# Gate and attention as one loop: a larger head start for the gate products, fewer of them per item, stored heads loaded three items ahead, and ScalarE's order written out

## The chip, the cores and the metric

The kernel runs on one core of one Trainium2 chip. The metric is the device time of one execution in microseconds (us). The core has TensorE (PE; its weight loads are shown as PEld), VectorE (DVE), ScalarE (ACT), GpSimd (POOL) and SyncE (SP), which here only issues DMAs. Each works through its own queue in order and waits on semaphores that the others set.

## The reference, cut to what matters

One step of a model with two layers, for 128 context tokens and 512 latent tokens of width 2048. The change lies in layer 0, the attention layer, and in the vectors for layer 1:

```
shift, scale, gate = split(silu(cond) @ w_mod[l] + b_mod[l])        # 2 condition rows
h = rms_norm(y, g_pre[l]) * (1 + scale) + shift
q, k, v, g = split(h @ w_in, [2048, 2560, 3072])                    # 16 heads of q, 4 of k and v
q, k = rope(rms_norm(q)), rope(rms_norm(k))                         # per head of 128
o = softmax(q @ [cache_k, k].T * HEAD_DIM ** -0.5) @ [cache_v, v]
out = (o * silu(g)) @ w_out                                         # g: one gate value per attention output
```

Latent tokens attend over 768 keys (256 cached and 512 of their own), context tokens over 128. Everything is float32.

## The kernel before

**Precision.** A float32 operand is split into two float32r parts. `split_w` casts a weight tile on ScalarE (L178, `wh`) and takes the difference on VectorE (L179, `wl`); both parts come out of a ring with a few slots. A product is then three float32r matmuls (`mm3`, L183 to L185). The activations lie in `hi` and `lo`, 128 x 16 x 642 each.

**Order.** Weights come through a ring of `raw` tiles of 1 MB, loaded by SyncE; a load waits until the last reader of its slot is done. TensorE follows the program's order inside the merged loop (`manual_schedule`). The other engines' queues are set by a scheduler that goes by priorities, and `split_w` asks for a high one.

**Ahead of the loop.** The gemms for k and q (`gemm_nat`) end with the last column blocks of q at 434 us. `gemv(0, ...)` runs in the background there. It accumulates the layer-1 shift on VectorE (L393, L395) in blocks of 1024 columns. At each of the two block ends, 16 float32 matmuls of 128x2 with `sel` (L402, 32 records in the trace) turn the sums over partitions into columns, and VectorE adds the bias (L409).

**The merged loop (L722 to L759).** `gate()` is a generator of 1536 products of 322 columns (L544): 16 heads, two halves of the tokens, two halves of the weights, 8 row blocks, three parts. It loads the gate weights of one head (L519) and calls `split_w` twice per head. `fill(n)` takes n products from it. The attention goes over 72 items: 16 heads by 4 blocks of 128 latent tokens, and after every odd head one item for the context tokens of two heads. Item n of the loop does the scores of item n and their softmax (`stage_s`: maximum L614, exponential L617, scaling L622 on ScalarE or L624 on VectorE), FILL[0] products, the weighted values of item n-2 (`stage_v`), FILL[1] products, the transposes of item n-1 (`stage_t`: L659, cast L662, difference L663), and FILL[2] products. Ahead of item 0, LEAD products are taken, all but 12 of them before the key and query transposes of head 0 (L576, L603). LEAD + 25 per item ends the gate with item 59.

**Where the results go.** `put_y` multiplies the attention output with the gate (L685). While the gate still runs, `hi` and `lo` hold its input, and a finished head is stored to DRAM (`a_s`, L699 on POOL's queue): heads 0 to 12. When it has ended (`over`), `put_y` writes `hi` on ScalarE (L687) and `lo` on POOL (L688) directly: heads 13 to 15. `load_a`, once per item from then on, brings one stored head back: load (L710), copy to `hi` on ScalarE (L711), difference to `lo` on POOL (L712). After the loop the output projection (`out_proj`) begins, a `gemm_nat` over `hi` and `lo` with `w_out_attn`, loaded by `load_w` (L169). Beside it, `gate_cols` sets its sums to zero on POOL (L773) and loads `w_mod`, `g_post` and `b_mod`.

## Time and profile before

| | us |
|---|---|
| three runs | 1981.70, 1983.51, 1984.18 |
| median | 1983.51 |
| the profiled execution | 1984.99 |
| its span in the trace | 1983.2 |
| TensorE busy in it | 1893.8 |

The profile is that of one execution. A line of order of time tells when an instruction started, how long it took and, in brackets, how long its engine had been idle before it and what ended that idle time. The table of windows cuts the span into stretches and tells for each how long every engine was busy and which TensorE clock was granted, as a share of full speed. Consecutive matmuls overlap in the records, so that the distance between starts, not the duration, tells what one costs. The loop starts after 434 us and the output projection starts at 910.92 us.

### The profile page before, as it was taken

The page shows a single profiled execution, that of the slowest core. Times are in us where ns is not written, and L with a number is a line of the kernel's source. Part 1 is how long each engine was busy: PE and PEld are TensorE (multiplying, and loading weights), DVE is VectorE, ACT ScalarE, POOL GpSimd, SP SyncE. Part 2 cuts the span into 40 slices and gives each one's busy share as a digit, 9 for nine tenths or more (in the row PEclk, how much of TensorE's full clock was granted, in tenths as well). Part 3 has the DMA queues.
Part 4 walks back from the last instruction along what each step waited for, and adds up shares of the span by engine and source line. Part 5 has one row for each costly group of instructions (what it writes and reads, how often), then busy time and mean ns, then how long its engine had stood idle before and what let it go on. Part 6 is the DMA issues. An engine that isn't in the chain of part 4 may idle for free.

```text
span 1983.2 us, 26998 instructions
## 1 busy us (share of the span) xinstructions
PE 1893.8 (95%) x10921; PEld 1693.3 (85%) x10921; DVE 1328.0 (67%) x1930; ACT 860.0 (43%) x1257; POOL 135.2 (7%) x215
## 2 busy tenths in 40 slices
PE   4999999998999999979999989999999999999997
PEld 1567888888999999977888889999999999987885
DVE  3237757848668685857867776775775674798645
ACT  4441222224444444463222555775365456642232
POOL 0000000000000000040000000100110010020000
PEclk9999999998999999999999989999999999999998
DMA  9995524624324252343555674322322322536445
GB/s 341 344 324 184 178 93 159 194 86 127 108 89 134 84 153 70 118 159 133 175 175 175 218 254 145 103 92 93 120 93 84 106 79 83 172 119 216 152 149 213
DMA packets 214701, 302.21 MB, mean 152 GB/s; under 512 B 7136, under 2 KB 140896, under 8 KB 211760
## 3 DMA queue, kind: packets, MB, share of 16 engines
q1 hardware_dynamic: 208848, 275.20, 42.8%
q0 software_dynamic: 5728, 25.28, 3.4%
q8 instruction: 86, 1.41, 0.3%
q14 instruction: 39, 0.32, 0.0%
HBM read 272.03 MB, written 28.42 MB: 151 GB/s over the span
## 4 chain that ended last, share of the span: by engine, by line
PE 75%; issue 11%; ACT 5%; DVE 5%; DMA 2%; SPq 1%; POOL 1%; DVEq 0%; ACTq 0%; POOLq 0%
PE pd L183 18%; PE pd L184 18%; PE pd L185 18%; PE pg L544 5%; PE pd L214 2%; PE pd L216 2%; PE pd L217 2%; PE pm L275 2%; PE pg L183 1%; ACT L976 1%; PE pg L185 1%; PE pg L184 1%; PE ph L659 1%; DVE wl L179 1%; PE ph L184 1%
## 5 line engine op out<-in xcount | busy, mean ns | idle before, releaser
L178 ACT CAST wh<-raw 128x1024 fp32r<-128x1024 f32 x248 | 258.7, 1048 | 527.8 <-PE pd L185 373.0
L179 DVE TENSOR_TENSOR wl<-raw,wh 128x1024 fp32r<-128x1024 f32 x248 | 301.9, 1221 | 218.4 <-ACT wh L178 217.2
L183 PE MATMUL pd<-wh,hi 128*128 128x512 f32 x1040 | 412.1, 396 | 8.0 <-ACT qf L485 3.8
L184 PE MATMUL pd<-wl,hi 128*128 128x512 f32 x1040 | 410.7, 395 | 0.0
L185 PE MATMUL pd<-wh,lo 128*128 128x512 f32 x1040 | 410.7, 395 | 0.0
L183 PEld LDWEIGHTS pd<-wh,hi 128*128 128x128 f32 x1040 | 196.1, 189 | 54.5 <-ACT qf L485 4.3
L183 PE MATMUL pd<-hi,wh 128*128 128x322 f32 x768 | 239.6, 312 | 0.0
L184 PE MATMUL pd<-lo,wh 128*128 128x322 f32 x768 | 238.4, 310 | 0.0
L185 PE MATMUL pd<-hi,wl 128*128 128x322 f32 x768 | 238.0, 310 | 0.0
L185 PEld LDWEIGHTS pd<-wh,lo 128*128 128x128 f32 x1040 | 196.1, 189 | 46.3
L184 PEld LDWEIGHTS pd<-wl,hi 128*128 128x128 f32 x1040 | 196.3, 189 | 45.4
L780 DVE SCALAR_TENSOR_TENSOR ga<-raw,cT,ga 128x512 f32<-128x512 f32 x256 | 175.5, 745 | 19.1 <-DMA ga<-b_mod 16.8
L395 DVE SCALAR_TENSOR_TENSOR ga<-raw,cT,ga 128x512 f32<-128x512 f32 (+1 forms) x180 | 162.5, 931 | 12.8 <-DMA raw<-w_mod 12.6
L544 PE MATMUL pg<-hi,wl 128*128 128x322 f32 x512 | 163.3, 319 | 0.0
L544 PE MATMUL pg<-lo,wh 128*128 128x322 f32 x512 | 162.9, 318 | 0.0
L544 PE MATMUL pg<-hi,wh 128*128 128x322 f32 x512 | 162.5, 317 | 0.0
L184 PEld LDWEIGHTS pd<-lo,wh 128*128 128x128 f32 x768 | 145.3, 189 | 0.0
L183 PEld LDWEIGHTS pd<-hi,wh 128*128 128x128 f32 x768 | 144.9, 189 | 0.1
L185 PEld LDWEIGHTS pd<-hi,wl 128*128 128x128 f32 x768 | 145.0, 189 | 0.0
L617 ACT ACTIVATE P<-sp,mx 128x768 f32<-128x768 f32 (+1 forms) x80 | 63.6, 797 | 98.3 <-DVE mx L614 98.3
L544 PEld LDWEIGHTS pg<-hi,wl 128*128 128x128 f32 x512 | 98.5, 192 | 0.0
L544 PEld LDWEIGHTS pg<-hi,wh 128*128 128x128 f32 x512 | 98.4, 192 | 0.0
(235 smaller groups left out, 3309.8 us busy)
## 6 DMA issues: line engine op xcount, KB each, us to landing
raw<-w_mod SPq DMA_DIRECT2D x64, 1024.0 KB, 5.2
raw<-w_in_lru SPq DMA_DIRECT2D x40, 1024.0 KB, 5.3
raw<-w_in_attn SPq DMA_DIRECT2D x36, 1024.0 KB, 5.8
raw<-w_mod SPq DMA_DIRECT2D x64, 512.0 KB, 8.1
raw<-w_out_attn SPq DMA_DIRECT2D x20, 1024.0 KB, 5.3
raw<-w_out_lru SPq DMA_DIRECT2D x20, 1024.0 KB, 6.1
y_s<-R POOLq DMA_DIRECT2D x16, 321.0 KB, 2.7
raw<-y_s SPq DMA_DIRECT2D x16, 321.0 KB, 4.2
```

The lines of the kernel that those rows point to most:

```text
L178: S.copy(wh, src)
L179: V.tensor_tensor(wl, src, wh.bitcast(F32), op=sub)
L183: PE.matmul(out, ah, bh, start=first, stop=False)
L184: PE.matmul(out, ah, bl, start=False, stop=False)
L185: PE.matmul(out, al, bh, start=False, stop=last)
L214: PE.matmul(outs[f], wh[:, c], hi[:, k, t], start=(k == 0 and first[f]), stop=False, skip_group_check=True)
L216: PE.matmul(outs[f], wh[:, c], lo[:, k, t], start=False, stop=False, skip_group_check=True)
L217: PE.matmul(outs[f], wl[:, c], hi[:, k, t], start=False, stop=(k == KT - 1), skip_group_check=True)
L395: V.scalar_tensor_tensor(acc[c], wk[:, k2], cT[:, k, c:c + 1], acc[c], op0=mult, op1=add)
L544: PE.matmul(acc[:, :TH], x[:, c], y[:, k, t], start=(q == 0 and k8 == 0 and n == 0), stop=(q == 1 and k8 == 7 and n == 2))
L617: S.activation(dst, src, AF.Exp, bias=mx[:, j:j + 1], accum_out=sm[:, j:j + 1])
L780: V.scalar_tensor_tensor(acc[:, c], raw[:, k4 * 512:k4 * 512 + 512], cT[:, kb * 4 + k4, c:c + 1], acc[:, c], op0=mult, op1=add)
```

## The change

Five edits:

- `LEAD` goes from 44 to 104 and `FILL` from (9, 8, 8) to (8, 8, 7). The gate then ends in the first fill of item 62 instead of with item 59, and one more head, 13, is stored and loaded back.
- `gemv(0, ...)` splits its two sums with `split_w` and takes 32 float32r matmuls (L405) in place of 16 float32 ones at each block end.
- `load_a` loads one stored head per item, up to three items ahead of the copy. It loads only heads that have been stored, and stops at the first head that went directly. With 14 stored heads, eight are copied in the rounds 65 to 72 of the loop over items, one in the last round, 73, and five in the loop behind it.
- ScalarE is added to `manual_schedule`: in the merged loop its queue is in the program's order too.
- The loop behind the items runs until nothing is left to load or copy.

```diff
--- before.py
+++ after.py
@@ -32,8 +32,8 @@
 QSCALE = HD ** -0.5
 NORM = "dadad"
 GGB = 5
-LEAD = 44
-FILL = (9, 8, 8)
+LEAD = 104
+FILL = (8, 8, 7)
 GATE2 = (1, 2, 5)
 GATE1 = (3, 4, 5, 6)
 NB1 = 2
@@ -397,10 +397,13 @@
                     if k2 % 2 or nk == 2:
                         yield
             pg = ps_()
+            parts = [split_w(a) for a in acc] if part == 0 else [(a,) for a in acc]
             for k in range(nf):
-                for c in range(2):
-                    PE.matmul(pg[:, 2 * k:2 * k + 2], acc[c][:, k * 128:k * 128 + 128],
-                              sel[:, c].bitcast(F32), start=(c == 0), stop=(c == 1))
+                ks = slice(k * 128, k * 128 + 128)
+                todo = [(a[:, ks], c) for c in range(2) for a in parts[c]]
+                for j, (a, c) in enumerate(todo):
+                    PE.matmul(pg[:, 2 * k:2 * k + 2], a, sel[:, c] if part == 0 else sel[:, c].bitcast(F32),
+                              start=(j == 0), stop=(j == len(todo) - 1))
             kt = col // 128
             src = pg[:, :2 * nf].rearrange("p (k c) -> p c k", c=2)
             b0 = 80 + part * 16 + kt
@@ -508,7 +511,7 @@
     def psh():
         return psH.tile([128, 512], F32, name="ph", tag="ph")
 
-    ggs, over, direct = {}, [], {}
+    ggs, over, direct, stored = {}, [], {}, set()
 
     def gate():
 
@@ -697,19 +700,25 @@
                 put_y(h - 1 + e, slice(PO, TE), po[:, e * 128:e * 128 + 128])
                 if not direct[h - 1 + e]:
                     G.dma_start(a_s[h - 1 + e][:, :TE], ggs[h - 1 + e][:, :TE])
-
-    back = iter(range(NH))
+                    stored.add(h - 1 + e)
+
+    coming, todo = [], list(range(NH))
 
     def load_a():
 
-        h = next(back, None)
-        if h is None or direct.get(h):
-            return
-        raw = rawp.tile([128, 2048], F32, name="raw", tag="raw")
-        r = raw[:, :TE]
-        SY.dma_start(r, a_s[h][:, :TE])
-        S.copy(hi[:, h, :TE], r)
-        G.tensor_tensor(lo[:, h, :TE], r, hi[:, h, :TE].bitcast(F32), op=sub)
+        if len(coming) == 3 or (coming and not todo):
+            h, r = coming.pop(0)
+            S.copy(hi[:, h, :TE], r)
+            G.tensor_tensor(lo[:, h, :TE], r, hi[:, h, :TE].bitcast(F32), op=sub)
+        if todo:
+            h = todo[0]
+            if h in direct and direct[h]:
+                todo.clear()
+            elif h in stored:
+                todo.pop(0)
+                raw = rawp.tile([128, 2048], F32, name="raw", tag="raw")
+                SY.dma_start(raw[:, :TE], a_s[h][:, :TE])
+                coming.append((h, raw[:, :TE]))
 
     items = []
     for h in range(NH):
@@ -719,7 +728,7 @@
     last = {h: (h, 4 if h % 2 else 3) for h in range(NH)}
     done = {}
     gv = gemv(1, pc_, psh, 512)
-    with tc.manual_schedule(engines={mybir.EngineType.PE}):
+    with tc.manual_schedule(engines={mybir.EngineType.PE, mybir.EngineType.Activation}):
         load_kv(0)
         load_q(0)
         fill(LEAD - 12)
@@ -755,7 +764,7 @@
                 load_a()
         for _ in gv:
             pass
-        for _ in range(NH):
+        while coming or todo:
             load_a()
     xs.close()
```

Three lines are added after L400, and more further on. L402 becomes L405, L409 L412, L544 L547, L687 L690, L688 L691, L710 L720 and L773 L782; L711 and L712 keep their numbers.

Three places show how the queues change. The first is VectorE at the second block end of `gemv(0, ...)`, just ahead of the loop. The `L179` rows from `raw` ahead of the `shift` row in the kernel before are the last weights of q and the first of the gate. Before:

```order
L179 TENSOR_TENSOR wl<-raw,wh 128x1024 x4
L458 TENSOR_REDUCE ss<-qs 128x8
L154 TENSOR_SCALAR rv<-ss 128x8
L156 RECIPROCAL rr<-ra 128x8
L157 TENSOR_TENSOR ra<-rv,rr 128x8
L158 TENSOR_TENSOR ra<-ra,rr 128x8
L409 TENSOR_TENSOR shift_151<-pd,VA 128x2x8
L159 TENSOR_SCALAR ra<-ra 128x8
L160 TENSOR_TENSOR rr<-rr,ra 128x8
L458 TENSOR_REDUCE ss<-qs 128x8
L179 TENSOR_TENSOR wl<-raw,wh 128x1024
L461 TENSOR_TENSOR qf<-qf,rr 128x1024
```

And changed:

```order
L179 TENSOR_TENSOR wl<-ga_2165,wh 128x1024
L179 TENSOR_TENSOR wl<-ga_2166,wh 128x1024
L461 TENSOR_REDUCE ss<-qs 128x8
L154 TENSOR_SCALAR rv<-ss 128x8
L156 RECIPROCAL rr<-ra 128x8
L157 TENSOR_TENSOR ra<-rv,rr 128x8
L158 TENSOR_TENSOR ra<-ra,rr 128x8
L159 TENSOR_SCALAR ra<-ra 128x8
L160 TENSOR_TENSOR rr<-rr,ra 128x8
L412 TENSOR_TENSOR shift_151<-pd,VA 128x2x8
L464 TENSOR_TENSOR qf<-qf,rr 128x1024
L179 TENSOR_TENSOR wl<-raw,wh 128x1024 x2
```

The two sums are split ahead of the matmuls, and the split of the gate's first weights (the `L179 ... x2` row) now stands behind the shift, which needs those matmuls.

The second place is ScalarE in the last items of the loop. Before, from item 66 on:

```order
L711 CAST hi<-raw 128x642
L606 CAST qh<-ph 128x512
L617 ACTIVATE P,sm<-sp,mx 128x768
L606 CAST qh<-ph 128x128
L622 ACTIVATE P<-P,rs 128x768
L687 CAST hi<-gg 128x256
L178 CAST wh<-raw 128x1024 x2
L662 CAST pth<-ph 128x3x128 x2
L617 ACTIVATE P,sm<-sp,mx 128x768
```

And changed, from item 70 to the output projection:

```order
L690 CAST hi<-gg 128x256
L665 CAST pth<-ph 128x3x128 x2
L711 CAST hi<-raw 128x642
L620 ACTIVATE P,sm<-sp,mx 128x128 x2
L665 CAST pth<-ph 128x3x128 x2
L711 CAST hi<-raw 128x642
L690 CAST hi<-gg 128x256
L671 CAST pth<-ph 128x256
L711 CAST hi<-raw 128x642
L690 CAST hi<-gg 128x128 x2
L711 CAST hi<-raw 128x642 x6
L178 CAST wh<-raw 128x1024 x6
```

Copies of stored heads now stand between the casts of one item and the exponential of the next, six more stand behind the last `put_y`, and the first casts of `w_out_attn` (L178), which stood among the items, come after all of these.

The third place is the entry to the output projection on SyncE, where the numbers of `a_s` count the stored heads from 78. Before:

```order
L710 DMA raw<-a_s_89 128x642
L592 DMA qx<-q_s 128x5x128
L710 DMA raw<-a_s_90 128x642
L169 DMA raw<-w_out_attn 128x4x512
L169 DMA raw<-w_mod 128x4x512 x2
L169 DMA raw<-w_out_attn 128x4x512
L169 DMA raw<-w_mod 128x4x512
L772 DMA gp<-g_post 128x512
```

And changed:

```order
L720 DMA raw<-a_s_88 128x642
L720 DMA raw<-a_s_89 128x642
L781 DMA gp<-g_post 128x512
L784 DMA ga<-b_mod 1x512
L720 DMA raw<-a_s_90 128x642
L720 DMA raw<-a_s_91 128x642
L169 DMA raw<-w_out_attn 128x4x512
L784 DMA ga<-b_mod 1x512
L169 DMA raw<-w_mod 128x4x512 x2
L169 DMA raw<-w_out_attn 128x4x512
```

On POOL, the differences that free the slots of those loads stood before the change in this order:

```order
L688 TENSOR_TENSOR lo<-gg,hi 128x128
L712 TENSOR_TENSOR lo<-raw,hi 128x642
L688 TENSOR_TENSOR lo<-gg,hi 128x256 x4
L688 TENSOR_TENSOR lo<-gg,hi 128x128 x2
L773 MEMSET ga 128x1024 x5
```

And changed:

```order
L691 TENSOR_TENSOR lo<-gg,hi 128x256
L712 TENSOR_TENSOR lo<-raw,hi 128x642
L691 TENSOR_TENSOR lo<-gg,hi 128x128 x2
L782 MEMSET ga 128x1024
L712 TENSOR_TENSOR lo<-raw,hi 128x642 x6
L782 MEMSET ga 128x1024 x4
```

The first load of `w_out_attn` moved from behind the last stored head inside the loop to behind fourteen of them. It goes into the slot of stored head 10, so it waits for the third of the six L712 rows that stand behind POOL's memset.

## Rows read from the trace of the kernel before

**Rows 1.** Part 1 of the page, over the whole span: engine, busy time, its share of the span, number of instructions.

```profile
PE 1893.8 (95%) x10921; PEld 1693.3 (85%) x10921; DVE 1328.0 (67%) x1930; ACT 860.0 (43%) x1257; POOL 135.2 (7%) x215
```

**Rows 2.** Busy time by window around the two ends of the merged loop. Columns: window, its length, then for each engine its busy time and instructions, then the granted TensorE clock as a share of full speed, the DMA share and the rate.

```profile
445.00:450.00 5.00, 0.12 (x1) 0.13 (x2) 4.83 (x12) 0.67 (x2) 0.71 (x1) 0.87 0.27 105
...
455.00:460.00 5.00, 0.69 (x3) 0.30 (x2) 5.00 (x7) 3.62 (x6) 3.05 (x2) 0.84 0.14 52
...
470.00:850.00 380.00, 380.00 (x2728) 379.23 (x2728) 279.57 (x518) 181.40 (x362) 15.13 (x17) 1.00 0.35 105
...
855.00:860.00 5.00, 0.67 (x7) 0.43 (x4) 2.44 (x5) 3.54 (x8) 4.49 (x4) 0.83 0.84 221
860.00:865.00 5.00, 3.55 (x13) 3.56 (x14) 2.82 (x5) 3.64 (x7) 5.00 (x4) 0.50 0.44 127
```

**Rows 3.** TensorE in order of time where the loop starts: start, duration, line, operation, and in brackets the idle time before it with its releaser.

```profile
434.21 3.63 PE L402 MATMUL pd<-sel,ga 128*128 128x2 f32 x32
...
439.07 0.47 PE L544 MATMUL pg<-lo,wh 128*128 128x322 f32 x1
439.34 0.47 PE L544 MATMUL pg<-hi,wl 128*128 128x322 f32 x1
...
442.28 0.31 PE L544 MATMUL pg<-hi,wl 128*128 128x322 f32 x1
442.43 0.31 PE L544 MATMUL pg<-hi,wh 128*128 128x322 f32 x1
...
449.88 0.90 PE L576 MATMUL ph<-ident,raw 128*128 128x128 f32 x3 [5.23 <-ACT qs L455]
...
457.23 0.45 PE L183 MATMUL sp<-kh,qh 128*128 128x384 f32 x1 [2.16 <-ACT qh L606]
...
461.12 0.69 PE L185 MATMUL sp<-kh,ql 128*128 128x384 f32 x1 [3.27 <-DVE ql L607]
...
462.57 0.47 PE L544 MATMUL pg<-hi,wl 128*128 128x322 f32 x1
```

**Rows 4.** TensorE in order of time, the same columns, near 304 us (first column block of the background product) and in the last part of the loop.

```profile
303.92 3.63 PE L402 MATMUL pd<-sel,ga 128*128 128x2 f32 x32
...
853.72 0.43 PE L183 MATMUL sp<-kh,qh 128*128 128x384 f32 x1
...
861.45 0.69 PE L183 MATMUL sp<-kh,qh 128*128 128x384 f32 x1 [5.78 <-ACT P L617]
...
867.23 0.27 PE L185 MATMUL sp<-kh,ql 128*128 128x128 f32 x1
867.34 0.28 PE L183 MATMUL sp<-kh,qh 128*128 128x128 f32 x1
...
870.12 0.44 PE L183 MATMUL sp<-kh,qh 128*128 128x384 f32 x1 [0.62 <-ACT P L617]
...
910.92 0.39 PE L183 MATMUL pd<-wh,hi 128*128 128x512 f32 x1
```

**Rows 5.** VectorE in order of time where the loop starts, the same columns.

```profile
437.88 0.18 DVE L409 TENSOR_TENSOR shift<-pd,VA 128x16 f32<-128x16 f32 x1 [3.10 <-PE pd L402]
...
439.38 1.22 DVE L179 TENSOR_TENSOR wl<-raw,wh 128x1024 fp32r<-128x1024 f32 x1
...
454.08 0.69 DVE L475 TENSOR_TENSOR qs<-qf,gain_q 128x512 f32<-128x512 f32 x1
...
456.57 3.89 DVE L395 SCALAR_TENSOR_TENSOR ga<-raw,cT,ga 128x512 f32<-128x512 f32 x3
460.39 0.88 DVE L607 TENSOR_TENSOR ql<-ph,qh 128x512 fp32r<-128x512 f32 x2
```

**Rows 6.** What TensorE waited for between 853 and 960 us: engine, tile and line that waited, what it waited for, total, times, longest.

```profile
PE sp L183 <- ACT P L617: 11.6, 5, 5.8
```

**Rows 7.** ScalarE in order of time in the last part of the loop.

```profile
882.17 0.73 ACT L711 CAST hi<-raw 128x642 fp32r<-128x642 f32 x1 [0.95 <-DMA raw<-a_s]
...
886.37 1.99 ACT L178 CAST wh<-raw 128x1024 fp32r<-128x1024 f32 x2
...
895.74 1.02 ACT L178 CAST wh<-raw 128x1024 fp32r<-128x1024 f32 x1
```

**Rows 8.** SyncE's queue of DMA issues in the last part of the loop.

```profile
879.18 0.32 SPq L710 DMA_DIRECT2D raw<-a_s  x1
879.59 0.39 SPq L169 DMA_DIRECT2D raw<-w_out_attn  x1
```

**Rows 9.** Groups by line and form between 845 and 915 us: line, engine, operation, tile, shapes and count, then busy time and mean ns of one, then the idle time before them.

```profile
L712 POOL TENSOR_TENSOR lo<-raw,hi 128x642 fp32r<-128x642 f32 x13 | 20.3, 1593 | 23.7 <-ACT hi L711 23.7
...
L711 ACT CAST hi<-raw 128x642 fp32r<-128x642 f32 x13 | 9.3, 728 | 5.6 <-DMA raw<-a_s 4.8 <-PE pg L544 0.6
...
L685 DVE SCALAR_TENSOR_TENSOR gg<-ph,gg 128x128 f32<-128x128 f32 x4 | 1.0, 283 | 0.6 <-PE ph L185 0.6
...
L773 POOL MEMSET ga<- 128x1024 f32 x1 | 1.0, 952 | 0.1
...
L687 ACT CAST hi<-gg 128x128 fp32r<-128x128 f32 x3 | 0.8, 297 | 1.1 <-DVE gg L685 1.1
```

**Rows 10.** DMA issues of the whole span, grouped: transfer, queue, count, KB each, median us from issue to landing.

```profile
raw<-w_out_attn SPq DMA_DIRECT2D x20, 1024.0 KB, 5.3
...
raw<-a_s SPq DMA_DIRECT2D x13, 321.0 KB, 4.2
```


## Prediction

> **What bounds the kernel now.** I read the page's busy times first, then a table of windows, then each engine in order of time at both ends of the merged loop. TensorE is busy for 1893.8 of 1983.2 us [rows 1], so the gain to be had is its idle and half-speed time. Inside the loop there is none: from 470 to 850 us it is busy in all 380.00 us at a clock of 1.00 [rows 2]. The losses lie at the loop's two ends. At the start it stands idle for 5.23 us before the key transposes, 2.16 us before the first scores and 3.27 us inside them [rows 3], 10.7 us in all, and the clock falls to 0.50 in parts [rows 2]. There a gate product costs 0.27 us from start to start instead of 0.15 us [rows 3]. At the end the gate has run out of products. TensorE waits 5.78 us for one softmax, then runs at 0.50 [rows 2, 4], and waits 11.6 us in all for ScalarE's exponentials and scalings [rows 6]. Both ends together cost some 30 us, which no change here can exceed as a gain. After the loop the output projection follows without any idle time [rows 4], because its first weights were issued at 879.59 us, 31 us ahead [rows 8].
>
> I take about 0.2%, 4 us, as what a measurement of this kernel can tell from no change.
>
> **Part 1, the block ends of the gemv.** TensorE gets 32 float32r matmuls for 16 float32 ones, which the trace shows as 32 records in 3.6 us [rows 3, 4], 0.11 us each. The nearest float32r rows are the 128x128 scores, also 0.11 us from start to start (867.23 to 867.34) [rows 4]. I take 3.5 us, no difference; the bounds are 3.5 us and, if only the columns counted, under 1 us. But the sums are split through the same ring as the gemm's weights, so the weights of the next piece are split behind VectorE's shift, which waits for these matmuls. Near 304 us TensorE then waits for the shift (0.18 us) and one split (1.22 us) [rows 5], less the two products that it has: 0.9 us lost.
>
> On weight loads, the Trainium skill, TensorE: Matmul & The Clock Gate, section on weight-path perf modes, states that a fast weight load is on when there are 128 weights and the type is not FP32. By that rule float32r loads might be faster than those of the old matmuls; the equal 0.11 us of the two kinds of rows speaks against it. The sum without the rule keeps 3.5 us; with it, it would be that of the second rival.
>
> **Part 2, the start of the loop.** The matmuls of the second block end start at 434.21 and end near 437.7 us, as before. The gate's first weights now come behind the shift at 437.88, a multiplication of the same 128x1024 elements and the split: 437.9 + 0.2 + 1.2 + 1.2 = 440.5 us. TensorE has two products to do until then and is idle for 2.5 us. It then runs at half speed for as long as after the 5.78 us wait (861.45 to about 865) or a little longer; to 445 us that makes 17 products at 0.27 us. The other 73 of the 92 products ahead of the transposes follow at 0.148 us until 455.9 us. The keys' transposes, which it waited for until 449.88 before, are ready then, so that wait is filled with products.
>
> The next limit is VectorE. Its chain for the last q block ended at 454.77 (454.08 + 0.69) [rows 5]; one more split ahead of it makes that about 456.0. From there to the end of the queries' low parts (460.39 + 0.88 = 461.27) it took 6.5 us. Now two more accumulations, one operation of the gate and one split stand in between. An accumulation is between 0.69 us, like the other 128x512 operation there, and 1.3 us, a third of the 3.89 us; the gate's 322 columns take under 0.69, and the split 1.22. That adds 3.1 to 4.5 us; against it the difference for the values on POOL, beside which the 3.89 us stood, moves to later, which takes off up to 1.8 us. So the queries are ready at 463.8 to 467.0, the first scores end about 0.9 us later, and I take 465.5 us. Before, they ended at 462.57 [rows 3] with 44 products done, now with 104. Sixty products at 0.148 us are worth 8.9 us, 2.9 us are lost: a gain of 6.0 us, or **5.1 us** with part 1. Bounds: 2.5 us with the late end of VectorE's chain, 7.5 us with the early end and no loss near 304 us.
>
> **Part 3, the middle.** Two products fewer per item leave more of a wait uncovered, and ScalarE in program order may hold an exponential behind a cast. ScalarE is busy for 181 of 380 us there and VectorE for 280 [rows 2], and TensorE has no idle time, so I take 0; the bounds are 0 and 4 us lost.
>
> **Part 4, the last items.** Before, items 60 to 62 ran without gate products, from 853.72 to 870.12 us, with 6.4 us idle and 3.6 us at half speed, which costs 1.8: 8.2 us [rows 4]. Now the gate reaches into item 62 and covers them; its products themselves only moved. From item 63 on there are eight copies on ScalarE in place of one (7 x 0.73 = 5.1 us [rows 9]), and none of the three casts of weights (1.99 + 1.02 us [rows 7]). They stand ahead of the exponentials that TensorE waits for, so I add the 2.1 us. The gain is **6.1 us**. Bounds: 2 us, where copies also wait for their loads as the one at 882.17 did [rows 7], and 10 us, where copies are hidden.
>
> **Part 5, the entry to the output projection.** This is the new wait. The first load of its weights takes the slot of stored head 10 and waits on SyncE for that head's difference on POOL. That is the third of six that stand behind the last `put_y` and a memset. Let T be the end of the last weighted values (before, the first product of the projection at 910.92 took over there with no idle time). Two multiplications on VectorE 0.56 us, two casts on ScalarE 0.6, the two differences of 128x128 on POOL about 0.9 us and the memset 0.95 [rows 9], overlapping in part, end at T + 2.9. Three differences at 1.56 us (20.3 over 13) [rows 9] make it T + 7.6. The load lands 5.3 us later [rows 10], T + 12.9; its cast on ScalarE, behind all six copies, 1.0 us, and the low part for the second product bring about T + 14.4. The six copies (4.4 us) and their loads are done by T + 11 and don't set the end. TensorE is idle for all of it, since the projection is all that its queue holds there. Then comes the half clock of 3.6 us, 1.8 lost. Together **16.2 us lost**. Bounds: 14 us, if the load lands in the 4.2 us of a stored head and the clock holds; 18 us, if the casts and loads queue. The load was free before, since it was issued 31 us ahead; that cover is gone. Later weights follow behind the first and are taken up at the gemm's pace, so I count them at nothing.
>
> **Sum.** 1984.99 - 5.1 - 6.1 + 16.2 = 1990.0 us for the profiled execution. It lies 1.5 us above the median of the runs, so against the median the forecast is 1983.5 + 5.0 = **1988.5 us**.
>
> **The rivals.**
>
> - *The end of the loop loses its waits altogether: faster.* Before, four waits besides the 5.78 us one make up 5.8 us of the 11.6 us [rows 6], 0.62 of it counted in part 4. If ScalarE's program order puts each exponential where it is wanted, and the copies, whose loads now run three items ahead, fit between, the last items gain 8.2 + 5.2 = 13.4 us instead of 6.1. With the early end at the start (7.5) it gives 1983.5 - 13.4 - 7.5 + 16.2 = 1979 us. It decides if the waits of TensorE for exponentials from item 63 on sum to under 1 us. For it: the loads came late for one copy in rows 7. Against it: the copies stand ahead of exponentials in the queue. 17%.
> - *The float32r matmuls are short.* At under 1 us instead of 3.5, both block ends and all that follows on VectorE come 2.5 us sooner: 1988.5 - 5 = 1983.5 us, no change. Against it: the 0.11 us of float32r rows. 10%.
> - *The middle is no longer covered: slower still.* With 23 products and ScalarE in order, a wait of 0.1 us in each of 60 items makes 6 us more, 1994 us. Against it: the idle shares of part 3. 15%.
> - *The forecast*, 1982 to 1994 us with the bounds of its terms mostly drawn together: 58%. Gains and loss of like size stand against each other in it, so it reaches into no change for about a quarter of its cases.
>
> **How the numbers follow.** Slower by over 0.2%: 0.41 of the forecast's 0.58 and 0.14 of the third rival's: 0.55. Within 0.2%: 0.16 of the forecast, 0.08 of the second rival, 0.04 of the first and 0.01 of the third: 0.29. Faster: 0.13 of the first, 0.02 of the second and 0.01 of the forecast: 0.16. The range from 1979 to 1996 us takes in the second rival, most of the third and the better part of the first's edge; about 2 in 10 stay outside.
>
> **What the changed profile would show.** Part 1: L405 with 32 records near 3.5 us, and about 1 us of idle time behind it near 307 us. Part 2: no wait before the key transposes (now L579), and the first scores done near 465 us. Part 3: no idle time from 470 to 870 us. Part 4: item 62 reached at full clock, waits for exponentials afterwards. Part 5: the first product of the projection waiting some 14 us, on its weights' cast behind the DMA, then half clock. I am wrong if that wait is under 8 us, or if the two ends of the loop together give back over 16 us.

## The result

| | runs | median us | lowest to highest |
|---|---|---|---|
| before | 4 | 1982.61 | 1981.40 to 1984.18 |
| changed | 4 | 1994.14 | 1992.48 to 1998.74 |

The changed kernel is slower by 11.5 us at the median; the ratio is 1.0061, with a 95% interval from 1.0043 to 1.0080 (ratios here are worked out over all runs and need not be the quotient of two medians). The profiled execution of it took 1993.89 us, with a span of 1992.1, 8.9 us over the span of before.

Windows of the changed kernel come first, with the columns of [rows 2].

```profile
445.00:450.00 5.00, 5.00 (x36) 5.00 (x36) 4.97 (x9) 0.60 (x1) 0.00 (x0) 1.00 0.28 108
...
480.00:850.00 370.00, 366.69 (x2638) 364.79 (x2637) 276.06 (x512) 174.95 (x356) 13.97 (x16) 1.00 0.36 108
855.00:860.00 5.00, 4.80 (x35) 4.24 (x34) 3.70 (x10) 2.83 (x10) 0.00 (x0) 1.00 0.22 66
...
870.00:875.00 5.00, 5.00 (x23) 4.90 (x22) 3.00 (x6) 1.84 (x4) 0.49 (x1) 0.50 0.25 69
...
905.00:910.00 5.00, 0.00 (x0) 0.00 (x0) 0.00 (x0) 2.41 (x4) 4.94 (x6) 0.50 0.53 142
910.00:915.00 5.00, 0.00 (x0) 0.00 (x0) 0.00 (x0) 1.45 (x2) 5.00 (x4) 0.50 0.83 266
```

The hole before the key transposes (445 to 450 us) is filled: TensorE was busy for 0.12 us of it in [rows 2] and is busy for all 5 now. The hole at 855 to 860 us is filled too. In their place TensorE does nothing at all from 905 to 915 us, and from 480 to 850 us, where it had no idle time, it now misses 3.3 us. TensorE in order of time at the places of [rows 3] and [rows 4]:

```profile
305.27 0.79 PE L184 MATMUL pd<-wl,hi 128*128 128x512 f32 x1 [0.61 <-DVE wl L179]
...
437.65 0.64 PE L547 MATMUL pg<-hi,wl 128*128 128x322 f32 x1 [1.81 <-DVE wl L179]
...
452.94 0.92 PE L579 MATMUL ph<-ident,raw 128*128 128x128 f32 x7
...
456.67 0.38 PE L547 MATMUL pg<-hi,wh 128*128 128x322 f32 x1 [1.66 <-ACT kh L581]
...
458.38 0.41 PE L547 MATMUL pg<-hi,wl 128*128 128x322 f32 x1 [1.18 <-DVE wl L179]
...
462.49 0.53 PE L185 MATMUL sp<-kh,ql 128*128 128x384 f32 x1
...
856.48 0.43 PE L183 MATMUL sp<-kh,qh 128*128 128x384 f32 x1
```

The 0.61 us near 305 us and the 1.81 us before the third gate product, the first one that takes a low part (`wl`), are the waits for splits that moved behind the shift. The transposes (L579) start at 452.94 without a wait, and the first scores' last product starts at 462.49, where in the kernel before the next gate product starts at 462.57 [rows 3]: the same time, with sixty products more behind it.

The entry to the output projection, TensorE:

```profile
903.52 0.42 PE L185 MATMUL ph<-pth,vl 128*128 128x256 f32 x1
917.83 1.22 PE L183 MATMUL pd<-wh,hi 128*128 128x512 f32 x2 [13.89 <-ACT wh L178]
```

SyncE's issues there, in the columns of [rows 8]:

```profile
908.24 1.82 SPq L720 DMA_DIRECT2D raw<-a_s  x2
911.23 0.38 SPq L169 DMA_DIRECT2D raw<-w_out_attn  x1
```

POOL:

```profile
904.84 0.87 POOL L691 TENSOR_TENSOR lo<-gg,hi 128x128 fp32r<-128x128 f32 x2
905.77 0.95 POOL L782 MEMSET ga<- 128x1024 f32 x1
906.68 9.02 POOL L712 TENSOR_TENSOR lo<-raw,hi 128x642 fp32r<-128x642 f32 x6
```

ScalarE:

```profile
904.71 1.98 ACT L711 CAST hi<-raw 128x642 fp32r<-128x642 f32 x3
907.88 0.73 ACT L711 CAST hi<-raw 128x642 fp32r<-128x642 f32 x1 [1.20 <-DMA raw<-a_s]
911.09 0.73 ACT L711 CAST hi<-raw 128x642 fp32r<-128x642 f32 x1 [2.48 <-DMA raw<-a_s]
912.62 0.73 ACT L711 CAST hi<-raw 128x642 fp32r<-128x642 f32 x1 [0.80 <-DMA raw<-a_s]
916.73 1.99 ACT L178 CAST wh<-raw 128x1024 fp32r<-128x1024 f32 x2 [3.39 <-DMA raw<-w_out_attn]
```

Read from below: TensorE's 13.89 us end with the cast of the weights (L178, 916.73), that had waited for the DMA, issued at 911.23. The DMA waited for POOL's third difference (906.68 plus three times 1.5 us, 911.2), which stood behind the memset. The last weighted values ended about 903.94 (917.83 less the idle time). The load was issued 7.3 us behind that, against 31 us ahead of the projection before [rows 8].

**Where the 8.9 us came from.** Both traces are cut at the same places: the start of the block end (L402, L405), the first score product of items 1, 60 and 63, the end of the last weighted values, the projection's first product, the end. As the two kernels have done different numbers of gate products at a cut, each missing one is counted at 0.148 us, as in the prediction. "Start" is from the block end to item 1, "middle" from item 1 to item 60. The rows beside that of the changed kernel belong to the experiments of the next section. Differences to the kernel before in us (to within 0.1), positive for lost, one profiled execution each:

| kernel | up to the block end | start | middle | items 60 to 62 | item 63 to the last values | wait at the projection | behind its first product | sum |
|---|---|---|---|---|---|---|---|---|
| changed | -2.7 | -6.0 | 4.2 | -9.1 | 6.7 | 13.9 | 2.0 | 8.9 |
| e1_scalar_free | -0.8 | -2.6 | 1.2 | -6.8 | 5.2 | 0 | -1.3 | -5.1 |
| e2_lead_fill_only | 1.7 | -5.5 | 1.3 | -6.8 | 7.9 | 0 | 1.3 | -0.1 |
| e3_fp32_block_end | -2.4 | -8.9 | 3.9 | -9.1 | 5.6 | 14.8 | 2.2 | 6.0 |
| e4_old_loads | -0.7 | -6.0 | 3.0 | -9.1 | 5.6 | 7.7 | 1.6 | 2.1 |
| e5_first_weights_early | 0.8 | -6.0 | 4.0 | -9.1 | 6.8 | 0 | 10.4 | 6.8 |
| e6_best_in_order | -2.6 | -10.2 | 5.0 | -9.1 | 7.0 | 0 | 2.8 | -7.0 |
| e7_scalar_order_only | -2.5 | -3.1 | 4.2 | -4.5 | 9.8 | 0 | 3.0 | 6.8 |
| e8_order_at_start_only | 0.3 | -8.8 | 2.6 | -6.6 | 6.6 | 0 | 1.3 | -4.7 |
| e9_order_to_round_61 | 0.6 | -6.1 | 4.1 | -6.8 | 5.6 | 0 | -1.3 | -3.8 |
| e10_copies_shared | -1.4 | -8.9 | 4.9 | -8.5 | 8.4 | 0 | 1.8 | -3.6 |
| e11_before_order_to_59 | 1.4 | -3.1 | 4.2 | -0.3 | 0.9 | 0 | -1.8 | 1.3 |

As an example, "start" of the changed kernel: item 1 starts 36.05 us behind the block end with 127 products done, before 33.51 us with 69; 2.54 less 58 times 0.148 is -6.0. The first column scatters between -2.7 and 1.7 us though nothing was edited in most of that stretch: e2, whose program up to there is that of the kernel before, has 1.7. It is scatter between executions, and so is part of the difference between a profile's sum and the medians below. Most of the changed kernel's 2.7 us lies in one wait of TensorE near 150 us (1.75 us instead of 3.83) and in the granted clock, which fell to 0.50 for 3.4 us behind that wait in the kernel before and not in the changed one.

### The profile page after: what moved, and what is told of

Same layout as the page of the kernel before. It is cut to its first block, busy times and chain, and to the rows that moved or that the text cites. A ratio compares the mean times of both kernels' runs of the same rounds, so it can differ in the third digit from the quotient of the medians.

```text
span 1992.1 us, 26946 instructions
## 1 busy us (share of the span) xinstructions
PE 1898.6 (95%) x10921; PEld 1694.1 (85%) x10921; DVE 1337.2 (67%) x1934; ACT 860.3 (43%) x1259; POOL 134.8 (7%) x214
## 4 chain that ended last, share of the span: by engine, by line
PE 82%; DVE 7%; ACT 6%; DMA 3%; issue 1%; SPq 1%; POOL 0%; DVEq 0%; ACTq 0%
PE pd L183 18%; PE pd L184 18%; PE pd L185 18%; PE pg L547 9%; PE pd L214 2%; PE pd L216 2%; PE pm L275 2%; PE pd L217 2%; PE ph L662 2%; DVE ga L395 1%; PE pg L183 1%; PE ph L184 1%; PE ph L183 1%; DMA raw<-w_mod 1%; PE ph L185 1%
## 5 line engine op out<-in xcount | busy, mean ns | idle before, releaser
L178 ACT CAST wh<-raw 128x1024 fp32r<-128x1024 f32 x248 | 258.6, 1048 | 489.8 <-PE pd L185 348.9
L179 DVE TENSOR_TENSOR wl<-raw,wh 128x1024 fp32r<-128x1024 f32 x248 | 301.4, 1221 | 208.8 <-ACT wh L178 207.6
L183 PE MATMUL pd<-wh,hi 128*128 128x512 f32 x1040 | 412.7, 397 | 19.3 <-ACT wh L178 13.9
L395 DVE SCALAR_TENSOR_TENSOR ga<-raw,cT,ga 128x512 f32<-128x512 f32 (+1 forms) x180 | 161.5, 929 | 14.6 <-DMA raw<-w_mod 14.4
L547 PE MATMUL pg<-hi,wl 128*128 128x322 f32 x512 | 163.2, 319 | 3.0 <-DVE wl L179 3.0
L547 PE MATMUL pg<-hi,wh 128*128 128x322 f32 x512 | 163.1, 319 | 1.7 <-ACT kh L581 1.7
L547 PE MATMUL pg<-lo,wh 128*128 128x322 f32 x512 | 162.2, 317 | 0.0
L547 PEld LDWEIGHTS pg<-hi,wl 128*128 128x128 f32 x512 | 98.0, 191 | 3.7 <-DVE wl L179 3.7
L547 PEld LDWEIGHTS pg<-hi,wh 128*128 128x128 f32 x512 | 98.2, 192 | 1.9 <-ACT kh L581 1.9
```

Of the source, the lines that this page charges most:

```text
L178: S.copy(wh, src)
L179: V.tensor_tensor(wl, src, wh.bitcast(F32), op=sub)
L183: PE.matmul(out, ah, bh, start=first, stop=False)
L395: V.scalar_tensor_tensor(acc[c], wk[:, k2], cT[:, k, c:c + 1], acc[c], op0=mult, op1=add)
L547: PE.matmul(acc[:, :TH], x[:, c], y[:, k, t], start=(q == 0 and k8 == 0 and n == 0), stop=(q == 1 and k8 == 7 and n == 2))
```

## The experiments

The theory after the result (A): ScalarE's program order causes the wait at the entry and most of the loss from item 63 on. The rival (B): the later end of the gate, with one stored head more and fewer items left, causes them. All medians here stand beside those of the kernel before on the same chip, 1983.1 to 1983.3 us.

**e1_scalar_free.** One edit to the changed kernel:

```diff
-    with tc.manual_schedule(engines={mybir.EngineType.PE, mybir.EngineType.Activation}):
+    with tc.manual_schedule(engines={mybir.EngineType.PE}):
```

> The changed kernel with ScalarE's order left to the scheduler in the merged loop; all else as changed. Theory A (ScalarE's program order causes the entry wait of 13.9 us and most of the 6.7 us lost from item 63 on): the first load of w_out_attn is issued inside the loop again, the projection starts without a wait, but the copies come in a burst at items 62 to 64 and cost about 8 us there: 1980 us, 14 us under the changed kernel. Rival B (the losses come from the later end of the gate and the fourteenth stored head, whatever ScalarE's order): 1990 us or more, with a wait of over 8 us left at the projection's entry.

Measured: 1981.14 us, ratio to the kernel before 0.9998 (0.9987 to 1.0010). The entry wait is gone, as A has it. But item 63 to the last values still loses 5.2 of the 6.7 us, so that part of A failed, and the start gains only 2.6 us. What TensorE waited for between 433 and 470 us, in the columns of [rows 6]:

```profile
PE pg L547 <- DVE gg L551: 5.4, 1, 5.4
```

VectorE's gate operation frees an accumulator there. Ahead of it stand three accumulations of the gemv, beside POOL's difference for the values; VectorE and POOL in e1:

```profile
457.50 4.39 DVE L395 SCALAR_TENSOR_TENSOR ga<-raw,cT,ga 128x512 f32<-128x512 f32 x3
461.82 0.47 DVE L551 SCALAR_TENSOR_TENSOR gg<-gg,pg 128x322 f32<-128x322 f32 x1
```

```profile
457.93 2.08 POOL L590 TENSOR_TENSOR vl<-raw,vh 128x896 fp32r<-128x896 f32 x1
```

And the same three accumulations in the changed kernel, where the written order has the values' cast, and with it POOL's difference, later (at 478 us):

```profile
454.05 2.07 DVE L395 SCALAR_TENSOR_TENSOR ga<-raw,cT,ga 128x512 f32<-128x512 f32 x3
```

The order takes 2.3 of its 3.4 us at the start from this.

**e2_lead_fill_only.** The kernel before with two numbers:

```diff
-LEAD = 44
-FILL = (9, 8, 8)
+LEAD = 104
+FILL = (8, 8, 7)
```

> The kernel before with LEAD and FILL alone changed. Theory A: the start's gain of 6 us and a few us of the middle's loss, no entry wait, the burst of copies moved to items 62 to 64: 1977 to 1981 us, 2 to 6 us under the kernel before. Rival B: 1988 us or more, slower than the kernel before by over 5 us.

Measured: 1981.65 us, ratio 0.9987 (0.9974 to 1.0001), just short of a clear gain and 0.65 us above A's range. B is out: the later end of the gate alone brings no entry wait. The 6.8 us that items 60 to 62 gain come back behind item 63 as 7.9 us; 3.4 of them are lost in item 63, among the copies, the others further on (see part 4 below).

**e3_fp32_block_end.** The changed kernel with the old matmuls at the block ends:

```diff
-            parts = [split_w(a) for a in acc] if part == 0 else [(a,) for a in acc]
+            parts = [(a,) for a in acc]
...
-                    PE.matmul(pg[:, 2 * k:2 * k + 2], a, sel[:, c] if part == 0 else sel[:, c].bitcast(F32),
+                    PE.matmul(pg[:, 2 * k:2 * k + 2], a, sel[:, c].bitcast(F32),
```

> The changed kernel with the old 16 float32 matmuls at the two block ends of gemv part 0, no split. Theory A: the gate's first weights are ready when the block end is done, so that the waits of 1.8 us near 437 us and 0.6 us near 305 us go, and the first scores come 1 to 3 us sooner; the entry wait stays at 14 us: 1991 to 1993 us. Rival B for this term (VectorE's long chain sets the first scores whatever the split): no change, 1994 us.

Measured: 1993.88 us, ratio 1.0054 (1.0035 to 1.0074), 0.3 us under the median of the changed kernel. In the trace, the start gains 8.9 us instead of 6.0, so the split costs 2.9 us there; the medians, four runs from 1991.1 to 1996.2, don't resolve it, and by the median alone B's number came. The same 2.9 us stand between e1 (2.6) and e2 (5.5), which differ in the split and in the loads alone.

**e4_old_loads.** The changed kernel with the `load_a` of before, which loads and copies one head per round from the gate's end on, so that each copy comes three rounds sooner, and three stand behind the last `put_y` instead of six.

```diff
+    back = iter(range(NH))
+
     def load_a():
 
+        h = next(back, None)
+        if h is None or direct.get(h):
+            return
+        raw = rawp.tile([128, 2048], F32, name="raw", tag="raw")
+        r = raw[:, :TE]
+        SY.dma_start(r, a_s[h][:, :TE])
+        S.copy(hi[:, h, :TE], r)
+        G.tensor_tensor(lo[:, h, :TE], r, hi[:, h, :TE].bitcast(F32), op=sub)
```

> The changed kernel with the old load_a (load, copy and difference of one stored head together, one head per item), ScalarE still in program order. Theory A: each copy stands in ScalarE's order right behind its own load, but SyncE can still issue loads ahead as slots come free, so loads mostly land in time; the entry wait stays above 8 us since the copies are as late: 1988 to 1996 us. Rival B (the loads three items ahead are what keeps items 63 to 71 going): copies wait for loads of 4 to 5 us in several items, 2000 us or more.

Measured: 1987.80 us, ratio 1.0026 (1.0012 to 1.0040), 6.3 us under the changed kernel. B is out; A had slightly more time (from 1988 us) and a longer wait (over 8 us) than came. What TensorE waited for between 850 and 950 us:

```profile
PE pd L183 <- ACT wh L178: 7.7, 1, 7.7
```

The wait goes from 13.9 to 7.7 us with fewer copies left over, and items 63 to 71 lose no more than before (5.6 against 6.7 us). So the loads three items ahead brought nothing here; that they delay the copies by three rounds cost some 6 us.

**e5_first_weights_early.** The changed kernel with the first weights of the projection loaded in round 67 and split in rounds 70 and 71:

```diff
+            if n == 67:
+                first = load_w(i["w_out_attn"][0], 0, 4, 0, 512)
+            if n in (70, 71):
+                ready.append(split_w(first[:, (n - 70) * 1024:(n - 69) * 1024]))
...
-            raw = load_w(w, kb * 512, 4, col0, 512)
+            raw = None if ready else load_w(w, kb * 512, 4, col0, 512)
...
-                wh, wl = split_w(raw[:, half * 1024:half * 1024 + 1024])
+                wh, wl = ready.pop(0) if raw is None else split_w(raw[:, half * 1024:half * 1024 + 1024])
```

> The changed kernel, with the first load of w_out_attn issued in round 67 of the loop and its two halves split in rounds 70 and 71, so that the projection starts with 14 us of products in hand. Theory A (the 13.9 us wait and the half clock behind it are the price of that one load's place): the wait goes; the second load still stands behind the six copies and comes 0 to 3 us late: 1978 to 1983 us. Rival B (the projection can't go on without the copies behind the loop, so the wait only moves to the second load): over 8 us of wait are left, 1988 us or more.

Measured: 1992.68 us, ratio 1.0046 (1.0028 to 1.0063). This expectation failed: B's number came, with 7.0 us of waits rather than over 8. SyncE and then TensorE:

```profile
885.70 0.38 SPq L169 DMA_DIRECT2D raw<-w_out_attn  x1
...
911.91 1.86 SPq L722 DMA_DIRECT2D raw<-a_s  x2
...
918.07 0.37 SPq L169 DMA_DIRECT2D raw<-w_out_attn  x1
```

```profile
907.35 0.63 PE L183 MATMUL pd<-wh,hi 128*128 128x512 f32 x1
...
928.08 1.65 PE L183 MATMUL pd<-wh,hi 128*128 128x512 f32 x3 [5.71 <-ACT wh L178]
```

The first load is issued at 885.70 and the projection starts at 907.35 without a wait. But the second load can't leave before 918.07, since it waits for a slot behind the same copies, and lands beside three others of 1 MB (two issued 3.1 and 1.5 us ahead of it, one 1.5 us behind): its cast starts at 926.98. After 15 us of products TensorE waits again, 5.7 us for the high part and 1.3 us for the low, and goes through the half clock twice. The part behind the first product loses 10.4 us. What blocks the entry is not one load's place but the copies behind the loop, through which every slot has to pass.

**e6_best_in_order.** e3, e4 and e5 together, with ScalarE in program order.

> Three undoings together, ScalarE still in program order: float32 matmuls at the block ends, the old load_a, the first weights of the projection early. If the terms read from the runs so far add up (start 8.9 us gained, middle 3.7 lost, items 60 to 62 9.1 gained, items 63 to 71 5.6 lost, entry 0 to 2 lost): 1974 to 1977 us, 6 to 9 us under the kernel before. If they don't add up (the early weights take what the copies need): 1980 us or more.

Measured: 1980.22 us (ten runs, 1973.95 to 1985.46), ratio 0.9987 (0.9970 to 1.0003). In the profile the terms add up: the start gains 10.2 us and there is no wait at the entry; its span is 7.0 us under that of before. But by the median, 3 us under the kernel before, the other expectation came (1980 us or more), and the interval reaches no change.

**e7_scalar_order_only.** The kernel before, with ScalarE in `manual_schedule` as the one edit.

> The kernel before with ScalarE in program order as the only edit. Theory A (the entry wait needs both: the order and copies that are left over behind the loop): thirteen copies from round 60 on are done inside the loop, so the first load of w_out_attn is freed in time and the projection starts with under 3 us of wait; the middle loses 3 us, the burst of copies at items 60 to 62 spreads out: 1981 to 1986 us. Rival B (the order alone is what delays the load): a wait of over 8 us, 1990 us or more.

Measured: 1991.90 us, ratio 1.0044 (1.0028 to 1.0060). Here A's sum failed, though not for B's reason: there is no wait at the entry, and still the kernel loses three quarters of what the whole change loses (8.6 of 11.5 us). Waits of TensorE between 850 and 960 us, and ScalarE there:

```profile
PE sp L183 <- ACT P L617: 5.8, 4, 1.9
PE ph L183 <- ACT pth L662: 4.6, 1, 4.6
```

```profile
902.17 1.99 ACT L178 CAST wh<-raw 128x1024 fp32r<-128x1024 f32 x2 [0.71 <-DMA raw<-w_out_attn]
...
905.11 0.74 ACT L711 CAST hi<-raw 128x642 fp32r<-128x642 f32 x1
```

One copy per item now stands ahead of the next exponential (905.11), but TensorE's waits for exponentials sum to 5.8 us, less than the 11.6 us of before [rows 6]. Its longest wait is for the casts of the transposes: 4.6 us, against 1.9 us in the changed kernel. Ahead of these casts stand two of the projection's first weights (902.17), which waited 0.71 us for their DMA and took 1.99 us. The program has them behind the loop; the order written for the loop didn't keep them out of it. From item 60 to the last values the kernel loses 5.3 us (-4.5 + 9.8), behind the projection's start 3.0 us, in the middle 4.2 us.

**e9_order_to_round_61 and e11_before_order_to_59.** The new theory (C) has the order's cost in two places: 3 to 4 us in the middle, the rest from the gate's end on. Its rival (D) has it in the part that these two keep. The loop was cut in two, with ScalarE in program order in the first part alone:

```diff
+    with tc.manual_schedule(engines={mybir.EngineType.PE, act}):
...
+        rounds(0, 62)
+    with tc.manual_schedule(engines={mybir.EngineType.PE}):
+        rounds(62, len(items) + 2)
```

(e11: the kernel before, with 60 in place of 62.)

> The changed kernel with ScalarE in program order only up to round 61 of the loop, and the scheduler's order from there on; split, loads three ahead, LEAD and FILL as changed. Theory C (the order's cost lies in two places: 3 us in the middle, and some 14 us at and behind the projection's entry, since the scheduler would have run the copies in a burst and the first weights' cast ahead of the last items): the start and the middle stay as in the changed kernel, the entry wait goes: 1978 to 1982 us. Rival D (the order cost what it did through the head start and the middle, and the entry only showed it): 1988 us or more.

> The kernel before with ScalarE in program order up to round 59 and the scheduler's order from there on. Theory C: of what the order alone cost in the kernel before (8.6 us: start 3.1 gained, middle 4.2, items from 60 on 5.3 and the projection 2.9 lost), only the middle's loss and the start's gain stay: 1983 to 1986 us, within 2 us of the kernel before. Rival D: the loss is in the middle and stays, 1989 us or more.

Measured: e9 1980.63 us, ratio 0.9987 (0.9976 to 0.9998), 13.5 us under the changed kernel; e11 1985.94 us, ratio 1.0014 (1.0002 to 1.0026), 6.0 us under e7. Both as C has them, though e11 is 2.8 us above the kernel before, not within 2. The middle's loss stays (4.1 and 4.2 us), the end's goes.

**e8_order_at_start_only and e10_copies_shared.** The start gains by the order, so e8 keeps it up to round 2 and leaves the rest to the scheduler, with float32 matmuls at the block ends and the old `load_a`. e10 is e8 with the copies of odd heads on VectorE:

```diff
-        S.copy(hi[:, h, :TE], r)
+        if h % 2:
+            V.tensor_copy(hi[:, h, :TE], r)
+        else:
+            S.copy(hi[:, h, :TE], r)
```

> ScalarE in program order only up to round 2 of the loop, the scheduler's order behind; float32 matmuls at the block ends and the old load_a; LEAD and FILL as changed. If the terms add up (start 8.9 us gained by the order and the larger head start, middle 1.3 lost, burst of copies moved: 6.8 gained at items 60 to 62 and 5.2 lost behind, no entry wait): 1973 to 1976 us. If the start's gain needs the order further on: 1978 to 1982 us.

> Order at the start only (as in the run of that name), with the copies of the odd stored heads on VectorE in place of ScalarE. If the burst on ScalarE at items 62 to 66 is what costs the 5 to 7 us left at the end: half of it goes, 1974 to 1977 us, 2 to 4 us under that run. If VectorE or the differences on POOL bound those items: no change, 1977 to 1980 us.

Measured: e8 1978.39 us, ratio 0.9976 (0.9961 to 0.9991), 4.9 us under the kernel before and 15.8 under the changed one: it beats both. The time is the one expected if the start's gain needed the order further on, but the start keeps its gain (8.8 us): the sum was too low because the middle loses 2.6 us instead of 1.3 and the last items 6.6 instead of 5.2. e10 1978.95 us, ratio 0.9980 (0.9968 to 0.9993): no change to e8. What TensorE still waits for in e8 between 850 and 960 us:

```profile
PE sp L183 <- ACT P L620: 7.2, 3, 4.4
PE sp L183 <- ACT qh L609: 2.3, 1, 2.3
```

ScalarE and TensorE at the longest of these waits:

```profile
880.81 1.99 ACT L178 CAST wh<-raw 128x1024 fp32r<-128x1024 f32 x2 [1.30 <-DMA raw<-w_out_attn]
...
883.08 0.90 ACT L620 ACTIVATE P<-sp,mx 128x768 f32<-128x768 f32 x1
```

```profile
884.13 0.69 PE L183 MATMUL sp<-kh,qh 128*128 128x384 f32 x1 [4.37 <-ACT P L620]
```

Items 60 to 62 gain 6.6 us and the items behind lose the same 6.6 us. The longest wait is not at the copies: that exponential stands behind the casts of the projection's first weights, which waited for their load. Moving half of the copies to VectorE doesn't help (-8.5 and 8.4 in e10), so ScalarE alone isn't what bounds those items. In e10's trace TensorE has a new wait of 2.19 us before 861.01, for a low part on VectorE behind two scalings of 128x128 (L627) that took 2.22 us together, beside six differences of stored heads on POOL (851.80 to 861.51). Whether these differences, the loads' landing or VectorE's own order bounds the items was not tried.

## Why the prediction came out as it did

The direction and the range (1979 to 1996 us) held; the predicted 1988.5 us lies 5.6 under the measured median. The direction was right for the reason given, the wait at the entry. The size was not: 5.0 us of loss were predicted and 11.5 measured, and 1994.1 us is at the upper end of what the forecast allowed (1982 to 1994). Step by step, in the profiles:

- **Part 1, block ends: right.** The 32 float32r matmuls come 0.11 us apart, like the float32 records of before, so the rival of short float32r matmuls fell. With it falls, as a gain here, the rule of the Trainium skill that the prediction cites (TensorE: Matmul & The Clock Gate, section on weight-path perf modes). The wait near 305 us was 0.6 us; 0.9 was predicted. That the stretch up to the second block end came out 2.7 us shorter is scatter, and luck for the sum.
- **Part 2, the start: right.** 6.0 us were predicted and 6.0 measured. The first scores were done at 462.8 instead of 465.5 and the transposes came at 452.94 instead of 455.9, but the block end had come 2.7 us sooner: counted from it, the scores were done after 31.3 us, as predicted, and the transposes came after 21.5 instead of 21.7. The difference for the values on POOL moved away, as I had allowed for; VectorE had three more accumulations to do and not two, at 0.7 us each. Which edits make it up came out only in the runs: 5.5 us of it are the larger head start (e2), the order adds 3.4 (e1 against the changed kernel), the split takes 2.9 (e3).
- **Part 3, the middle: size and mechanism were wrong.** I took 0 with a bound of 4 us, by a wait left uncovered or an exponential held behind a cast; it lost 4.2, and the waits in it are of another kind. Without the written order (e1) the middle loses 1.2 us, so the order makes 3 us of it. The waits of TensorE between 480 and 850 us:

```profile
PE ph L183 <- DVE ptl L666: 3.0, 2, 2.3
```

  Two waits for the low part of transposed attention weights (`ptl`) make up 3.0 us, the longer one 2.27 us, before the weighted values at 597.18. VectorE and POOL ahead of it:

```profile
590.64 0.75 DVE L395 SCALAR_TENSOR_TENSOR ga<-raw,cT,ga 128x512 f32<-128x512 f32 x1 [1.58 <-DMA raw<-w_mod]
...
591.38 2.55 DVE L395 SCALAR_TENSOR_TENSOR ga<-raw,cT,ga 128x512 f32<-128x512 f32 x1
```

```profile
591.00 2.38 POOL L590 TENSOR_TENSOR vl<-raw,vh 128x896 fp32r<-128x896 f32 x1 [5.16 <-ACT vh L589]
```

  An accumulation of the gemv took 2.55 us instead of 0.75 while POOL took its difference for the values, and VectorE had no pause from there to the low part (596.58); the added 1.8 us make up most of the wait. The other wait, 0.70 us before 481.43, is alike; a scaling of 128x768 (L627) on VectorE, which takes 0.62 us otherwise, beside the first such difference in the loop:

```profile
477.76 0.73 DVE L395 SCALAR_TENSOR_TENSOR ga<-raw,cT,ga 128x512 f32<-128x512 f32 x1
478.42 2.50 DVE L627 TENSOR_SCALAR P<-P,rs 128x768 f32<-128x768 f32 x1
```

```profile
478.39 2.10 POOL L590 TENSOR_TENSOR vl<-raw,vh 128x896 fp32r<-128x896 f32 x1 [23.93 <-ACT vh L589]
```

  In e4, with the same order, the scaling kept its 0.62 us beside that difference, which took 2.61 us instead, and the wait near 481 us is gone (e3 and e6: 0.2 us left):

```profile
480.47 0.62 DVE L627 TENSOR_SCALAR P<-P,rs 128x768 f32<-128x768 f32 x1
```

```profile
480.45 2.61 POOL L590 TENSOR_TENSOR vl<-raw,vh 128x896 fp32r<-128x896 f32 x1 [23.98 <-ACT vh L589]
```

  The order moved these differences to where VectorE has such work. In e7 and e11, TensorE's waits of 1.06 and 2.30 us in the middle follow differences on POOL too (L624 2.50 us ahead of the first; ahead of the second an accumulation of up to 1.7 us, which explains at most 1 us of it), and e8 and e10, where the scheduler orders the middle, have one wait of 2.0 us behind such a scaling (2.46 us). In e1, e2 and the kernel before, POOL's four differences fall beside shorter or unhurried work in the middle, and no such wait is there. So a part of the cost hangs on where POOL's difference falls, and the written order is one way to make it fall badly. What is left of the middle's loss beyond the waits, 0.5 to 1.1 us, stays open (2.3 us in e10, where the granted clock was also at 0.50 for 3.4 us behind its wait).
- **Part 4, the last items: the step that failed most.** Items 60 to 62 gave 9.1 us (8.2 predicted). For the items behind I added 2.1 us of copies and it was 6.7. Windows from the first score of item 63 to the end of the last weighted values, in the changed kernel and then in the kernel before:

```profile
856.48:903.94 47.46, 38.36 (x226) 33.82 (x224) 27.36 (x59) 27.16 (x60) 15.49 (x14) 0.84 0.23 70
```

```profile
870.12:911.08 40.96, 33.64 (x224) 30.46 (x225) 28.61 (x61) 25.50 (x56) 6.20 (x8) 0.96 0.42 151
```

  TensorE idles 1.8 us more (9.1 against 7.3 us), close to the 2.1 us that I had added. The larger part is that the same products keep it busy for 4.7 us longer, at a mean granted clock of 0.84 instead of 0.96. So the term that I had wrong is the clock, for which I counted nothing there. Waits of TensorE between 850 and 960 us in the changed kernel:

```profile
PE pd L183 <- ACT wh L178: 13.9, 1, 13.9
PE sp L183 <- ACT P L620: 4.0, 3, 1.7
PE ph L183 <- ACT pth L665: 1.9, 1, 1.9
```

  The waits for exponentials make 4.0 us, no more than the 5.2 us of before (11.6 [rows 6] less 5.78 and 0.62 [rows 4]); the wait for the casts of the transposes, 1.9 us, is new. The clock fell to 0.50 just ahead of item 66, in 16 matmuls of 128x2 (L405) behind a wait of 0.9 us, until 875 us (window 870 to 875), and again at 896 us, in that wait of 1.9 us.

  In every kernel with the larger head start, these items lose 5.2 to 8.4 us, in whatever order the copies go, so the loss of [rows 4] wasn't filled for good. It doesn't come back in one place. With the written order, as in the changed kernel, it lies mostly in item 66 (3.2 us) and behind the start of item 71 (4.4 us). With the scheduler's order (e1, e2, e8, e9), 3.2 to 3.8 us lie in item 63, among the copies, and 2.8 to 3.6 us in items 67 and 68, where an exponential stands behind the casts of the projection's first weights. Whether one cause lies behind both is not shown. Over both columns the changed kernel gains 2.4 us, e1 1.6, e8 nothing, and e2 loses 1.1.
- **Part 5, the entry: right, term by term.** T + 7.3 us for the issue (7.6 predicted), T + 12.8 for the cast's start (12.9), T + 13.9 for the first product (14.4), and 2.0 us behind it (1.8). Its cover was named rightly; its cause is wider than one load, as e5 shows.

The sum of the misses: 4.2 in the middle and 3.7 in part 4, less 3.6 up to the block end (2.7 sooner instead of 0.9 later), less 0.3 in part 5, and rounding, make the 3.9 us between 5.0 and 8.9. The medians differ by another 2.6 us. That is about the 2.7 us by which the profiled execution was shorter up to the block end, and within the scatter between executions (the changed kernel's four runs span 6.3 us).

Of the rivals, the third (middle not covered) had the right place and two thirds of its size, but not the mechanism: not 0.1 us in each item, but three waits in 60 items, 2.27 us the longest. It came beside the forecast rather than in place of it, and that the measured time is close to its 1994 us comes from the other terms as much. The first (waits at the end gone) had its test, under 1 us of waits for exponentials from item 63 on, answered with 4.0.

## What to carry to other kernels

An order written out for one engine also fixes where its queue stands at the next stage: before doing so, list what comes behind the last piece of work in that order and which loads need its buffers, since every load whose slot is freed by that work moves with it. Work that a hole hides (here copies behind the gate's end) is not gone when the hole is filled: look for where it goes next, and count its cost there as it was before, until a run shows otherwise. Count with each new wait what the granted clock takes behind it: in the last items here that was more (4.7 us) than the added idle time (1.8 us). If an order helps in one stretch, write it out for that stretch alone (e8: three rounds of 74).

## What the runs showed of the hardware that was not expected

- Operations of VectorE on SBUF alone that started just behind the start of a difference of 128x896 on POOL (2.1 to 2.4 us) were mostly stretched: an accumulation of 128x512 took 2.55 us instead of 0.75, a scaling of 128x768 2.50 instead of 0.62. Both ended 0.4 to 0.6 us behind POOL's end (593.93 against 593.38, 480.92 against 480.49), as if they had waited for it. In e3, e4 and e6 it was the other way round: the scaling took 0.61 to 0.62 us and the difference 2.60 to 2.61. Three accumulations took 4.39 us in e1 and 3.89 us in [rows 5] in that company, and 2.07 us without it. This pair of engines decides a part of the start and of the middle. The Trainium skill, GPSIMD Engine Reference, section Specifications, states that POOL's SBUF interfaces are shared with VectorE and contend with its instructions of two SBUF inputs or in a 2-port performance mode; the rows here agree for the accumulations, and which mode the scaling runs in no run here shows.
- The records of float32r and of float32 matmuls of 128x2 stand 0.11 us apart alike, but each float32 matmul shows as two: 32 float32r matmuls and 16 float32 ones both cost 3.5 to 3.6 us, so splitting an operand to leave float32 brought nothing for products this narrow, and cost two splits.
- A load of 1 MB that was issued 1.5 us behind one such load and ahead of another took 8.9 us to its cast in e5 (918.07 to 926.98), against 5.3 us as the median of such loads [rows 10].
